# A planned decoder step: a margin before TensorE's side work, casts and copies fixed to ScalarE, more staging tiles, two stores on another queue

## The chip, the cores and the metric

The kernel runs on one core of a Trainium2 chip. A core has five engines, each with its own instruction queue, worked off in order: TensorE (PE, matrix multiplications into PSUM), VectorE (DVE), ScalarE (ACT), GpSimd (POOL) and SyncE (SP, which here only issues DMAs). The metric is the device time of one execution in microseconds (us). Before the change the median of three runs is 1080.3 us (1076.1 to 1082.3).

## The reference, cut to what matters

The reference computes one inference step of a two-layer recurrent decoder, in float32, for a prompt of 512 tokens and for 8 samples of one token each (520 columns in all), with a model width of 1024.

- Layer 0: RMSNorm, an input projection, and two branches. Branch A is a width-4 convolution, two block-diagonal gates and a linear recurrence (RG-LRU), times a SiLU gate. Branch B is a convolution with SiLU over x, B and C, a chunked state-space scan (SSD) with a step size dt per head, a SiLU gate z and a group norm. Both are concatenated and go through an output projection, then a residual add.
- Layer 1: RMSNorm, projections q, f, v and gate, a chunked linear-attention scan over 16 heads (HGRN2), a head norm, a SiLU gate, an output projection and a residual add.
- Each layer ends with a gated embedding:

```
def per_layer_embed(h, p, w_proj, w_gate):
    gate = jax.nn.sigmoid((h @ w_gate).astype(F32))
    return h + (gate * (p @ w_proj).astype(F32)).astype(h.dtype)
```

- A final RMSNorm gives y. Beside y the kernel returns the new recurrent and convolution states of prompt and samples.

## The kernel before, in words

**Layout.** Features lie on the 128 partitions and the 520 tokens (512 of the prompt, 8 samples) along the free dimension. A row of 128 features by 520 tokens is the unit of nearly all elementwise work.

**Multiplications.** Each float32 operand is split into two parts of a reduced type, a high one (cast) and a low one (the rest), and a product is three multiplications: high by high, high by low, low by high. A weight unit is 128 rows of contraction by 8, times 128 columns; `split_unit` makes its `whi` with a cast (by ScalarE or VectorE) and its `wlo` with a subtraction on VectorE. Both have two buffers. Weights come in by DMA two units at a time (`wraw`). `project` then runs one output row: for each of eight contraction steps a block of six multiplications, 48 in all, into a PSUM tile with two buffers, and then the row's evacuation.

**The planner.** The kernel's functions don't issue instructions; they record operations in a `Plan`. Main blocks (the projections) have a fixed order, and a position that grows by 0.668 us with each block. Everything else gets a due time: the position of its place in the code, shifted by a constant (`side(start, rate)`), and never later than what its main consumer needs. `Plan.order` then simulates all engines with a table of costs: an instruction becomes ready when its predecessors have ended (`release` adds `SYNC`, 0.12 us, between engines), and each engine takes the ready one that is due first. `copy` and `scaled` are recorded in two forms, one for ScalarE and one for VectorE, and the planner takes whichever engine comes free first. The result is a fixed order per engine. On the chip an engine that reaches an instruction whose operands are late stands still, and what is queued behind it waits too.

**TensorE's side work in layer 0.** Between the main blocks of the projections ax, xbc, z and ag stand:
- `gates(j)`: row j of xa, the convolution's result, is split into `xg`, and 12 multiplications with `gw` go into the PSUM tiles g;
- `ssd_start`: `dt_project` (multiplications, then transposes dtT), then on GpSimd a polynomial for the logarithm and the products dt and dA (tiles `htmp`, `dtt`), then the multiplications acs (cumulative sums) and the transposes acsT; `lru_out` transposes the last recurrence states (`ah`, from `ahs`);
- `ssd_chunk(g, c)`: for two groups and four chunks, transposes bt and xk, multiplications yd and yo, and the chunk's state st.

**Evacuation of ax and xbc.** `evac_raw` copies the PSUM row into a raw row (part of tile `bcs`), and the convolution then runs one ScalarE and three VectorE operations on it.

**The embeddings.** `embed(layer, ...)` multiplies p with `w_proj` into eight rows (pl), copies each into a staging tile and stores it to DRAM (`pl_d`) by SP; the rows are read back later. Four staging tiles take turns in both layers. Embedding 1 runs between the last projection of layer 0 (pg) and the first of layer 1 (f), beside the norm that makes layer 1's input (`xh`, `xl`). Its staging is the place `xa`, which holds 4160 columns of float32, and there are 8 x 520 such columns; later the same place takes the states of layer 1 (`l1c`).

**The end.** `layer1_end` runs the last projection in two halves of the tokens, then scales the transposed rows (`ytk`) by the final norm and stores y: four stores of 256 KB in the second half, and one for the samples, all issued by SP.

Of the kernel before, what the change touches and what calls it, by code (L numbers as in the profile page):

```python
# [25 lines left out]
N = T + NS  # L26
HN = N // 2
D = 1024
KT = D // 128
# [10 lines left out]
SYNC = 0.12  # L40
# [62 lines left out]
class Buf:  # L103


    def __init__(self, pool, shape, dt, tag, name, bufs, space, born):
        self.pool, self.shape, self.dt, self.tag, self.name, self.bufs, self.space = pool, shape, dt, tag, name, bufs, space
        self.born, self.acc, self.used, self.dead, self.real = born, [], [], None, None
        self.left, self.bank = 0, None
# [90 lines left out]
class Op:  # L200


    def __init__(self, plan, prio, i):
        self.plan, self.prio, self.i = plan, prio, i
        self.forms, self.preds, self.soft, self.succ, self.bufs = {}, {}, {}, [], {}
        self.size, self.cols, self.wait, self.ready, self.taken, self.main = 0, 0.0, 0, 0.0, None, False
        self.pinned = plan.pinned


class Plan:  # L210
# [3 lines left out]
    def __init__(self, engines, pools, banks):  # L214
        self.engines, self.pools, self.banks = engines, pools, banks
        self.ops, self.slots, self.pos, self.open, self.gate = [], defaultdict(list), 0.0, None, None
        self.shift, self.rate, self.pinned = 0.0, 0.0, False


    def tile(self, pool, shape, dt, tag, name, bufs=1, space=SBUF):  # L220
# [21 lines left out]
    @contextmanager  # L242
    def side(self, start=0.0, rate=0.0, pinned=False):

        keep = self.shift, self.rate, self.pinned
        self.shift, self.rate, self.pinned = start, rate, pinned
        yield
        self.shift, self.rate, self.pinned = keep

    @contextmanager  # L250
    def together(self, *views):
# [96 lines left out]
    def order(self):  # L348
# [17 lines left out]
        def release(op, t):  # L366
            todo = [(op, t)]
            while todo:
                p, t_ = todo.pop()
                for s, hard in p.succ:  # L370
                    if hard:
                        s.ready = max(s.ready, t_ + (SYNC if p.forms and not ("pe" in p.forms and "pe" in s.forms) else 0))
                    s.wait -= 1
                    if not s.wait:
                        offer(s, todo)

        def offer(s, todo):
            if not s.forms:
                todo.append((s, s.ready))
            for e in s.forms:  # L380
                heapq.heappush(pend[e], (s.ready, s.i, s))
# [63 lines left out]
        while left:  # L445
# [16 lines left out]
            calls, c, func = op.forms[e]  # L462
            for b in need(op):
                i = min(range(len(banks)), key=lambda i: banks[i])
# [8 lines left out]
            else:  # L473
                if e == "pe":

                    c = c + 0.003 * len(calls) if cols[int(t / 3.41333) - 1] >= 3060 else 2.0 * c
# [45 lines left out]
GATE_LATE, GATE_RATE, LRU_LATE, DT_LATE = -0.77, 1.03, 13.0, -5.19  # L522
SSD_LATE, SSD_C, SSD_G, SSD_RATE = -5.66, 3.04, 5.84, 0.14
# [7 lines left out]
def hybrid_decode_step_kernel(ctx: ExitStack, tc: tile.TileContext, I, O, mode="both"):  # L531
# [18 lines left out]
    plans = [Plan(engines, pools, [f"ax{i}" for i in range(4)])]  # L550
    act, dve, pool, pe, sp = (Engine(plans, k) for k in ("act", "dve", "pool", "pe", "sp"))
    side, block = (lambda *a, **k: plans[-1].side(*a, **k)), (lambda *a: plans[-1].block(*a))

    def new(pool_, shape, tag, name, bufs=1, dt=F32):
        return plans[-1].tile(pool_, shape, dt, tag, name, bufs, {"psm": PSUM, "psa": PSUM, "drp": DRAM}.get(pool_, SBUF))
# [7 lines left out]
    def grab(name):  # L563

        return new("psa", [128, 512], "ax", name)

    def halves(ap):
        return ap.rearrange("p (a b) -> p a b", a=2)

    def ps520(ps):  # L570
        return ps[:, :, :HN]
# [4 lines left out]
    def tt(out, a, b, op, eng=dve):  # L576
        eng.tensor_tensor(out=out, in0=a, in1=b, op=op)
# [13 lines left out]
    def copy(out, in_):  # L591

        plans[-1].record(("act", "copy", (out, in_), {}), ("dve", "tensor_copy", (out, in_), {}))
# [6 lines left out]
    def slot(tag, name, shape=None, dt=F32):  # L600
        return new("lay", shape or [128, KT, N], tag, name, dt=dt)
# [5 lines left out]
    groups, units, sec = [], [], {}  # L607
# [19 lines left out]
    def split_unit(u, hi=None, lo=None, eng=dve):  # L627
        g, s, uc, kk = units[u]
        if g not in raw_of:
            load_group(g)  # L630
        v = raw_of[g][:, :, s:s + uc]
        if hi is None:
            hi = new("wp", [128, 1024], "whi", f"whi{u}", 2, F32R)
            lo = new("wp", [128, 1024], "wlo", f"wlo{u}", 2, F32R)
        hv = hi[:, :kk * uc].rearrange("p (k c) -> p k c", k=kk)
        lv = lo[:, :kk * uc].rearrange("p (k c) -> p k c", k=kk)
        with side(*((plans[-1].shift, 0.0, True) if plans[-1].pinned else (-SPLIT_AHEAD,))):
            copy(hv, v)
            tt(lv, v, hv.bitcast(F32), SUB, eng)
        split_of[u] = (hv, lv)  # L640

# [61 lines left out]
    def project(u, m, pair, kmap, evac, name):  # L703
        project_both([(u, m, evac, name)], pair, kmap)
# [96 lines left out]
    def P1(r, n=1):  # L801
        return pt[:, 0, r:r + n]
# [62 lines left out]
    def embed(layer, PP, stg):  # L865
        def mk(j):
            def f(ps):
                s = stg[:, j % 4 * N:(j % 4 + 1) * N]
                copy(halves(s), ps520(ps))
                sp.dma_start(out=pl_d[layer][j], in_=s)  # L870
            return f

        for j in range(8):
            u, m = (sec["proj1"] + j // 4, j % 4) if layer else (sec["proj0"] + j // 2, j % 2) if j < 4 else (sec["proj0b"], j - 4)
            project(u, m, PP, [0, 1], mk(j), f"pl{layer}{j}")
# [164 lines left out]

    def evac_raw(ps, i, lc):
        raw = raws[i % 2]
        copy(halves(raw[:, 3:3 + N]), ps520(ps))
        pool.tensor_copy(lc, raw[:, T:T + 11])
        return raw

    xa, lt = slot("xa", "xa"), slot("z", "lt")
# [32 lines left out]
    def evac_ax(j):  # L1080
        def f(ps):
            raw = evac_raw(ps, j, LCa[:, :, j])
            conv(raw, xa[:, j, :T], P1(24 + j), P1(16 + j), P1(8 + j), P1(j), P1(32 + j))
            s = xa[:, j, T:]
            ts(s, LCa[:, 3:, j], P1(24 + j), MUL, P1(32 + j), ADD, pool)
            for k in (2, 1, 0):
                stt(s, SCa[:, :, k, j], P1(8 * k + j), s, MUL, ADD)
            for i in () if j == 0 else (0, 1) if j == 1 else (j,):
                with side(GATE_LATE, GATE_RATE):
                    gates(i)  # L1090
        return f

# [133 lines left out]
                lru(0)  # L1226
    with side(LRU_LATE):
        lru(4)
    with side(DT_LATE):
        ssd_start()  # L1230
        lru_out()

# [151 lines left out]

    for c in range(NCH):
        for g in range(2):
            with side(SSD_LATE + c * SSD_C + g * SSD_G, SSD_RATE):
                ssd_chunk(g, c)
    for g in range(2):
        with side(SSD_LATE + NCH * SSD_C):  # L1390
# [161 lines left out]
    with side(CONV_LATE):  # L1552
        conv_states()
    pp1 = slot("w", "pp1", [128, 4160], F32R)
    embed(1, split_p(pk1[:, :1024], pk1[:NS, 1024:1280], pp1[:, :4 * N].rearrange("p (k n) -> p k n", k=4), 1),
          slot("xa", "plt1", [128, 4 * N]))

    split_unit(sec["f0"], pp1[:, 2080:3104], pp1[:, 3104:4128])
    if mode == "both":
# [412 lines left out]
    def layer1_end(pl1, ytk, ytk4, keep, pre):  # L1972
# [7 lines left out]
        for j in range(2, 8):  # L1980
            t, o = keep[j // 2 - 1], j % 2 * 2048
# [40 lines left out]
        for half, (sl, blocks) in enumerate(HALVES):  # L2022
            psr = grab(f"ssf{half}")
            n, c0, nb = sl.stop - sl.start, blocks[0], len(blocks)
            for j in range(8):
                u = u0 + j
                hw, lw = split_of[u]
                ps = mmps(f"pg1{j}{half}")
                for k in range(8):
                    with block(True):  # L2030
                        for i, (w, x) in enumerate(((hw, xh), (hw, xl), (lw, xh))):
                            pe.matmul(ps[:, 0, :n], lhsT=w[:, k, :], rhs=x[:, k, sl],
                                      start=(k == 0 and i == 0), stop=(k == 7 and i == 2))
                    plans[-1].pos += 0.334
                evac(half, j, ps, psr)
            stt(ss[:, c0:c0 + nb], psr[:, 8 + c0:8 + c0 + nb], 1.0 / D, ss[:, c0:c0 + nb], MUL, ADD)
            for i in blocks:
                pool.tensor_tensor(out=ss[:, i:i + 1], in0=ss[:, i:i + 1], in1=nhalf[:, :1], op=ALU.pow)
            for i in blocks[:2]:
                for c in range(0, D, 512):  # L2040
                    y = ytk[:, i, c:c + 512]
                    scaled(y, y, ss[:, i:i + 1])
                    sp.dma_start(out=O["y_p"][0, i * 128:(i + 1) * 128, c:c + 512], in_=y)
        scaled(ytk4[96:], ytk4[96:], ss[96:, 4:5])
        sp.dma_start(out=O["y_s"].rearrange("b o d -> (b o) d"), in_=ytk4[120:])

    layer1_fast()
    layer1_end(slot("xa", "pl1"), slot("w", "ytk", [128, 4160])[:, :4 * D].rearrange("p (i d) -> p i d", i=4),
# [54 lines left out]
```

## Time and profile before

| | before |
|---|---|
| median of 3 runs | 1080.3 us (1076.1 to 1082.3) |
| profiled execution, its own time | 1080.04 us |
| its span, first to last instruction | 1078.3 us |
| mean granted TensorE clock | 0.989 |
| busy: TensorE / VectorE / ScalarE / GpSimd | 1046.1 / 778.2 / 507.6 / 140.2 us |
| moved by DMA | 138.43 MB, 128 GB/s |

How to read the profile: an engine's busy time doesn't say that it does useful work at full speed; beside it stands the clock that TensorE was granted (1.00 is full). Idle time is put down to what ended it ("releaser"), an engine and the tile that it wrote. Since the planner's loop issues everything, lines have one number (510) and tiles tell the work apart. A row of a window's view gives the window, its length, then busy time and count of TensorE, weight loads, VectorE, ScalarE and GpSimd, then the clock, the share of the DMA engines and GB/s. A queue with a small q (SPq, ACTq) is an engine's own DMA issues or sequencer.

### The profile page before, as it was taken

To read this page: it belongs to the slowest core of one execution; us is meant where nothing else is said; L and a number is where in the kernel's file an instruction comes from. 1 tells how busy PE (TensorE), PEld (TensorE's weight loads), DVE (VectorE), ACT (ScalarE), POOL (GpSimd) and SP (SyncE) were. 2 spreads that over 40 slices of the span, in tenths; PEclk is the share of its full clock that TensorE was granted. 3 is DMA by queue.
4 is the path that set the end of the run, shared out by engine and by line. 5 is a ranking of instruction groups with operands and counts; after the bars stand their busy time and mean duration, and the time that the engine had idled before them with its cause. 6 is when DMAs were issued, how large, how long until landed. Compare 5 with 4: busy or idle time off the path is not lost.

```text
span 1078.3 us, 21240 instructions
## 1 busy us (share of the span) xinstructions
PE 1046.1 (97%) x8595; PEld 1024.8 (95%) x8595; DVE 778.2 (72%) x1532; ACT 507.6 (47%) x1191; POOL 140.2 (13%) x241
## 2 busy tenths in 40 slices
PE   9999889999999999999999999999999999999995
PEld 8899889799999999999999999999999999999995
DVE  6899788999996656774858676575766757667853
ACT  6587464635474212352455445334463344642453
POOL 4636655110000000100000000000000000000000
PEclk9999899999999999999999999999999999999997
DMA  8712153344685234563433433342442433335311
GB/s 272 246 40 79 48 185 126 99 147 147 199 264 203 82 106 131 164 192 106 130 112 111 116 112 118 91 150 87 116 130 85 139 103 110 99 82 206 118 40 44
DMA packets 130466, 138.43 MB, mean 128 GB/s; under 512 B 13704, under 2 KB 111128, under 8 KB 130344
## 3 DMA queue, kind: packets, MB, share of 16 engines
q1 hardware_dynamic: 130136, 136.93, 41.1%
q8 instruction: 69, 1.13, 0.4%
q14 instruction: 37, 0.30, 0.1%
q0 software_dynamic: 224, 0.06, 0.0%
HBM read 111.71 MB, written 25.44 MB: 127 GB/s over the span
## 4 chain that ended last, share of the span: by engine, by line
PE 82%; DVE 6%; POOL 5%; DMA 3%; ACT 2%; issue 1%; POOLq 0%; DVEq 0%; ACTq 0%
PE o L510 11%; PE g L510 9%; PE f L510 9%; PE v L510 9%; PE q L510 9%; PE pg L510 7%; PE ag L510 4%; PE oa L510 4%; PE ob L510 4%; PE z L510 4%; PE xbc L510 2%; POOL htmp L510 2%; PE ax L510 1%; PE A L510 1%; PE kv L510 1%
## 5 line engine op out<-in xcount | busy, mean ns | idle before, releaser
L510 DVE TENSOR_TENSOR wlo<-wraw,whi 128x1024 fp32r<-128x1024 f32 (+1 forms) x143 | 173.5, 1213 | 4.2 <-ACT whi L510 2.4
L510 ACT CAST whi<-wraw 128x1024 fp32r<-128x1024 f32 (+1 forms) x67 | 69.5, 1037 | 126.8 <-PE q L510 41.2
L510 POOL TENSOR_TENSOR at__1569<-at__1569,nhalf 128x4 f32<-128x4 f32 (+1 forms) x24 | 20.7, 861 | 502.6 <-DVE at__1569 L510 502.6
L510 DVE CAST whi<-wraw 128x1024 fp32r<-128x1024 f32 x76 | 52.5, 691 | 38.5 <-PE f L510 13.2
L510 PE MATMUL g<-xh,whi 128*128 128x260 f32 x256 | 55.8, 299 | 0.0
L510 PE MATMUL q<-xh,whi 128*128 128x260 f32 x256 | 53.2, 289 | 0.0
L510 PE MATMUL o<-oh,whi 128*128 128x260 f32 x256 | 52.6, 286 | 0.0
L510 PE MATMUL v<-xh,whi 128*128 128x260 f32 x256 | 52.1, 285 | 0.0
L510 PE MATMUL v<-xh,wlo 128*128 128x260 f32 x256 | 51.6, 283 | 0.0
L510 PE MATMUL o<-oh,wlo 128*128 128x260 f32 x256 | 51.5, 283 | 0.0
L510 PE MATMUL g<-xh,wlo 128*128 128x260 f32 x256 | 51.5, 283 | 0.0
L510 PE MATMUL g<-xl,whi 128*128 128x260 f32 x256 | 51.5, 283 | 0.0
L510 PE MATMUL o<-ol,whi 128*128 128x260 f32 x256 | 51.5, 283 | 0.0
L510 PE MATMUL q<-xl,whi 128*128 128x260 f32 x256 | 51.5, 282 | 0.0
L510 PE MATMUL v<-xl,whi 128*128 128x260 f32 x256 | 51.4, 282 | 0.0
L510 PE MATMUL q<-xh,wlo 128*128 128x260 f32 x256 | 51.4, 282 | 0.0
L510 PE MATMUL f<-xh,whi 128*128 128x260 f32 x240 | 50.8, 293 | 0.0
L510 PE MATMUL f<-xl,whi 128*128 128x260 f32 x240 | 48.3, 283 | 0.0
L510 PE MATMUL f<-xh,wlo 128*128 128x260 f32 x240 | 48.2, 282 | 0.0
L510 DVE SCALAR_TENSOR_TENSOR l1a<-q,lbt,l1a 128x260 f32<-128x260 f32 (+1 forms) x32 | 14.0, 480 | 44.2 <-PE q L510 44.2
L510 DVE SCALAR_TENSOR_TENSOR l1c<-l1d,l1c 128x128 f32<-128x128 f32 x128 | 41.0, 347 | 0.6 <-ACT l1c L510 0.6
L510 PE MATMUL xbc<-xnh,whi 128*128 128x260 f32 x192 | 40.5, 294 | 0.0
(504 smaller groups left out, 3359.3 us busy)
## 6 DMA issues: line engine op xcount, KB each, us to landing
wraw<-in_c_w_in_dram SPq DMA_DIRECT2D x32, 1024.0 KB
wraw<-in_ab_w_in_dram SPq DMA_DIRECT2D x15, 1024.0 KB
wraw<-in_ab_w_out_dram SPq DMA_DIRECT2D x8, 1024.0 KB
wraw<-in_ple_gate_dram SPq DMA_DIRECT2D x8, 1024.0 KB
l1c<-in_state_c_dram SPq DMA_DIRECT2D x16, 512.0 KB
out_dram<-l1c SPq DMA_DIRECT2D x16, 512.0 KB
wraw<-in_c_w_out_dram SPq DMA_DIRECT2D x8, 1024.0 KB
pl<-pl_d SPq DMA_DIRECT2D x2, 2080.0 KB
```

Source lines behind the costliest of these rows:

```text
L510: getattr(f, name)(*a, **k)
```

## The change

Four things:

1. A new context, `later(spare)`. Operations recorded inside it carry `spare`, and when the planner works out when such an operation on TensorE is ready, it adds `spare` us for every predecessor that doesn't run on TensorE. The gates get 0.5, `ssd_start` and `lru_out` 4.0, and the SSD chunks 1.0.
2. In layer 0, from section ax2 up to (not including) pg0, the cast of each weight unit is recorded for ScalarE alone. That takes in ax2, proj0, proj0b, the xbc sections, z, ag, z1, out0a and out0b. The raw copy of `evac_raw` is for ScalarE alone, too.
3. `embed` takes turns over as many staging tiles as its place holds, and embedding 1 gets a place of eight; embedding 0 stays at four.
4. Of the last five stores of y, the second half of token block 3 and that of the samples are issued by ScalarE.

```diff
-        self.pinned = plan.pinned
+        self.pinned, self.spare = plan.pinned, plan.spare
...
+    @contextmanager
+    def later(self, spare):
+
+        keep, self.spare = self.spare, spare
+        yield
+        self.spare = keep
...
-                        s.ready = max(s.ready, t_ + (SYNC if p.forms and not ("pe" in p.forms and "pe" in s.forms) else 0))
+                        lag = SYNC if p.forms and not ("pe" in p.forms and "pe" in s.forms) else 0
+                        if "pe" in s.forms and p.taken != "pe":
+                            lag += s.spare
+                        s.ready = max(s.ready, t_ + lag)
...
-            copy(hv, v)
+            if sec["ax2"] <= u < sec["pg0"]:
+                act.copy(hv, v)
+            else:
+                copy(hv, v)
             tt(lv, v, hv.bitcast(F32), SUB, eng)
...
-                s = stg[:, j % 4 * N:(j % 4 + 1) * N]
+                i = j % (stg.shape[1] // N)
+                s = stg[:, i * N:(i + 1) * N]
...
-        copy(halves(raw[:, 3:3 + N]), ps520(ps))
+        act.copy(halves(raw[:, 3:3 + N]), ps520(ps))
...
-                with side(GATE_LATE, GATE_RATE):
+                with side(GATE_LATE, GATE_RATE), plans[-1].later(0.5):
                     gates(i)
...
-    with side(DT_LATE):
+    with side(DT_LATE), plans[-1].later(4.0):
         ssd_start()
         lru_out()
...
-            with side(SSD_LATE + c * SSD_C + g * SSD_G, SSD_RATE):
+            with side(SSD_LATE + c * SSD_C + g * SSD_G, SSD_RATE), plans[-1].later(1.0):
                 ssd_chunk(g, c)
...
-          slot("xa", "plt1", [128, 4 * N]))
+          slot("xa", "plt1", [128, KT * N]))
...
-                    sp.dma_start(out=O["y_p"][0, i * 128:(i + 1) * 128, c:c + 512], in_=y)
+                    (act if i == 3 and c else sp).dma_start(out=O["y_p"][0, i * 128:(i + 1) * 128, c:c + 512], in_=y)
...
-        sp.dma_start(out=O["y_s"].rearrange("b o d -> (b o) d"), in_=ytk4[120:])
+        act.dma_start(out=O["y_s"].rearrange("b o d -> (b o) d"), in_=ytk4[120:])
```

More of the change, by code (lines that the diff above doesn't have):

```diff
@@ L216, in __init__ @@
         self.ops, self.slots, self.pos, self.open, self.gate = [], defaultdict(list), 0.0, None, None
-        self.shift, self.rate, self.pinned = 0.0, 0.0, False
+        self.shift, self.rate, self.pinned, self.spare = 0.0, 0.0, False, 0.0
     def tile(self, pool, shape, dt, tag, name, bufs=1, space=SBUF):
```

## The prediction

> **What bounds the kernel now.** I read the page's engine shares first, then busy time by stage, then TensorE's waits, and last the stretches around each wait. All times are us, and nearly every instruction carries line 510, the one loop that issues the plan, so I go by tiles.
>
> ```profile
> PE 1046.1 (97%) x8595; PEld 1024.8 (95%) x8595; DVE 778.2 (72%) x1532; ACT 507.6 (47%) x1191; POOL 140.2 (13%) x241
> PE 82%; DVE 6%; POOL 5%; DMA 3%; ACT 2%; issue 1%; POOLq 0%; DVEq 0%; ACTq 0%
> ```
>
> TensorE is the bound: 97% busy, 82% of the chain that ended last. None of its multiplications goes away, so only three things can shorten the run: its waits, its slow-clock stretches, and the tail after its last instruction. TensorE's waits, longest first (what waited, for what; total, times, longest):
>
> ```profile
> PE acs L510 <- POOL dtt L510: 4.8, 1, 4.8
> PE ah L510 <- POOL ahs L510: 2.7, 1, 2.7
> PE pl L510 <- ACT plt L510: 2.1, 1, 2.1
> PE st L510 <- ACT bcs L510: 1.9, 1, 1.9
> ```
>
> The fifth group is the gate multiplications g, waiting in five places (the bracket is TensorE's idle time just before):
>
> ```profile
> 50.81 1.59 PE L510 MATMUL g<-xg,gw 128*128 128x260 f32 x11 [1.86 <-DVE xg L510]
> 55.62 1.58 PE L510 MATMUL g<-xg,gw 128*128 128x260 f32 x11 [0.21 <-DVE xg L510]
> 62.22 1.59 PE L510 MATMUL g<-xg,gw 128*128 128x260 f32 x11 [1.29 <-DVE xg L510]
> 95.52 0.39 PE L510 MATMUL g<-xg,gw 128*128 128x260 f32 x1 [0.79 <-ACT xg L510]
> 96.38 1.59 PE L510 MATMUL g<-xg,gw 128*128 128x260 f32 x11 [0.47 <-DVE xg L510]
> ```
>
> All but pl are side instructions of layer 0 that stand in TensorE's queue, in front of main blocks that could have run, before their operands are there. A wait also costs clock. Busy time by stretch (TensorE, weight loads, VectorE, ScalarE, GpSimd; then granted clock, DMA share, GB/s):
>
> ```profile
> 60.00:90.00 30.00, 28.71 (x237) 27.80 (x236) 29.43 (x59) 28.56 (x50) 10.99 (x16) 1.00 0.24 71
> 116.50:122.00 5.50, 5.50 (x25) 5.32 (x26) 3.09 (x7) 1.03 (x4) 4.45 (x16) 0.50 0.05 14
> 149.40:152.90 3.50, 3.50 (x18) 3.50 (x18) 1.83 (x7) 3.50 (x10) 1.49 (x3) 0.53 0.41 158
> 462.00:468.00 6.00, 6.00 (x38) 5.98 (x39) 5.39 (x9) 5.20 (x9) 0.00 (x0) 0.72 0.54 201
> 195.00:320.00 125.00, 124.39 (x1043) 118.90 (x1042) 118.95 (x234) 67.00 (x236) 7.43 (x6) 1.00 0.55 174
> ```
>
> The last row gives the full pace: 1043 in 125 is 8.34 per us, 0.12 each. Against it, 116.5 to 122 (behind the acs wait, clock 0.50) did 25 instead of 45.9, a loss of 20.9 x 0.12 = 2.5. Behind the ah wait: 18 instead of 29.2, a loss of 1.3. Behind the pl wait: 38 instead of 50, a loss of 1.4. The other waits are 1.9 and shorter and I charge them no clock.
>
> **The change, part by part.** I make the sum against the profiled execution: 1080.0, of which 1078.3 is the span and 1.7 lies around it. The median of the runs is 1080.3, so the two agree.
>
> *The margin of 4.0 for acs, acsT, dtT and ah.* The planner counts a TensorE instruction ready 4.0 later than its operands by its own clock, so it fills that time with main blocks. What is late is GpSimd's chain from dt to dA:
>
> ```profile
> 95.81 0.78 POOL L510 TENSOR_SCALAR dtt<-dtt 128x80 f32<-128x80 f32 x1 [0.18 <-DVE dtt L510]
> 116.07 0.35 POOL L510 TENSOR_TENSOR dtt<-dtt,hb 128x80 f32<-128x80 f32 x1
> ```
>
> From 95.81 to 116.42 it takes 20.6, and TensorE reached acs 4.8 too early. The margin on dtT delays chain and consumer alike; the one on acs takes 4.0 from the wait, leaving 0.8. So -4.0 (ends: 0 if GpSimd falls behind by as much again, -4.8 if it runs freer). A rest of 0.8 is below every wait behind which I counted slow matmuls, so the 2.5 goes too. The ah wait of 2.7 is inside the margin: -2.7 and -1.3 (ends: 0 and -4.0 together). What is queued behind acs and ah is main xbc work; what waits for their results is the SSD chunks, and these have time, as the next term shows.
>
> [...]
>
> *The margins of 0.5 (gates) and 1.0 (SSD chunks).* Each g wait shrinks by 0.5 at most: 1.86, 0.21, 1.29, 0.79, 0.47 (4.6) become 1.36, 0, 0.79, 0.29, 0 (2.4), so -2.2 (ends 0 and -4.6). The st wait of 1.9 becomes 0.9: -1.0 (ends 0 and -1.9). In exchange the side chains get longer. Serially that is at most 3 x 4.0 for ssd_start and, for each of four chunks, st and the next yo at 1.0 each: 8. Their consumers:
>
> ```profile
> L510 DVE SCALAR_TENSOR_TENSOR bx<-bx,dcol,yd x32: 333/342/346, 184.0 to 253.7; 128x128 f32<-128x128 f32 x32
> L510 DVE SCALAR_TENSOR_TENSOR bx<-bx,zs x8: 693/696/699, 278.6 to 332.7; 128x520 f32<-128x520 f32 x8
> ```
>
> The last chunk's output is written at 253.7 and first used at 278.6. These 25 hold both, 20, so I cost the longer chains at nothing; with that cover gone the price would be what exceeds 25.
>
> *Casts and raw copies fixed to ScalarE.* From 40 to 320 (busy us, mean ns):
>
> ```profile
> sum 280.00, PE 265.12 PEld 255.13 DVE 249.10 ACT 164.11 POOL 93.83; mean PE 37.87 PEld 36.45 DVE 35.59 ACT 23.44 POOL 13.40
> L510 DVE CAST whi<-wraw 128x1024 fp32r<-128x1024 f32 x20 | 13.8, 690 | 1.7 <-PE ag L510 0.8 <-PE z L510 0.5
> L510 ACT CAST whi<-wraw 128x1024 fp32r<-128x1024 f32 x16 | 16.7, 1043 | 0.6 <-PE oa L510 0.3 <-PE xbc L510 0.2
> L510 DVE TENSOR_TENSOR wlo<-wraw,whi 128x1024 fp32r<-128x1024 f32 x36 | 44.2, 1228 | 2.1 <-ACT whi L510 1.9
> L510 DVE CAST whi<-wraw x1: 689/689/689, 74.0 to 74.0; 128x1024 fp32r<-128x1024 f32 x1
> L510 DVE CAST whi<-wraw x2: 694/722/749, 81.5 to 102.9; 128x1024 fp32r<-128x1024 f32 x2
> L510 DVE COPY bcs<-ax x4: 687/690/692, 41.8 to 66.9; 128x520 f32<-128x520 f32 x4
> L510 DVE COPY bcs<-xbc x6: 692/699/701, 109.5 to 174.3; 128x520 f32<-128x520 f32 x6
> L510 ACT COPY bcs<-xbc x6: 570/594/596, 102.4 to 180.7; 128x520 f32<-128x520 f32 x6
> ```
>
> Twenty casts and ten copies move. VectorE loses 13.8 + 4 x 0.69 + 6 x 0.70 = 20.8 and falls from 249.1 to 228.3; ScalarE gains 20 x 1.04 + 10 x 0.59 = 26.8 and rises from 164.1 to 190.9 of 280. A faster TensorE needs VectorE to do the same work in less time, and the row from 195 to 320 has it at 118.95 of 125; the relief pays for that. A weight unit is 48 multiplications, 5.8; with two buffers a cast and its subtraction have that long, and need 1.04 + 1.23 = 2.3 instead of 0.69 + 1.23 = 1.9, so 3.5 of slack remain. Only from 60 to 90 does ScalarE lack room: 28.6 of 30, plus two casts (those at 74.0 and 81.5) and the later two of the four ax copies, 3.3, gives 31.9. I charge the 1.9 that is too much as +2 (ends 0, if the planner moves other copies to VectorE, and +3.3).
>
> *Eight staging tiles for embedding 1.* With four, the fifth copy waits until the first store has landed:
>
> ```profile
> 447.89 2.88 PE pl L510 x24
> 451.72 9.40 DMA pl_d<-plt
> 461.22 0.59 ACT L510 COPY plt<-pl 128x520 f32<-128x520 f32 x1 [3.30 <-DMA pl_d<-plt]
> 461.87 1.83 PE pl L510 x12
> 463.69 12.92 PE f L510 x96
> 458.02 0.76 DVE L510 SCALAR_TENSOR_TENSOR n<-h,pt,acc 128x520 f32<-128x520 f32 x1
> 462.99 0.69 DVE L510 TENSOR_TENSOR xl<-sqt,xh 128x520 fp32r<-128x520 f32 x1
> ```
>
> The wait (2.1) and its slow clock (1.4) go: -3.5. Next late is the norm that feeds f: the ScalarE casts of xh, now queued behind the blocked plt copy, come free with it; VectorE then needs 0.76 + 0.69 = 1.45 for each of eight steps where f needs 12 x 0.12 = 1.44. They run level, so I give back 0.5: -3.0 (ends -2.1 and -3.5). The eight stores stay on SP in the same order and no longer wait for a tile; the state loads that reuse their place (l1c) wait for the last of them in both kernels.
>
> *Two y stores from ScalarE.*
>
> ```profile
> 1069.24 1.67 DVE L510 TENSOR_SCALAR ytk<-ytk,ss 128x512 f32<-128x512 f32 x3 [0.32 <-POOL ss L510]
> 1069.75 2.94 SPq L510 DMA_DIRECT2D out_dram<-ytk  x5
> 1071.00:1072.00 1.00, 0.00 (x0) 0.00 (x0) 0.00 (x0) 0.00 (x0) 0.00 (x0) 0.50 0.94 359
> ```
>
> SP issues five stores in 2.94, 0.59 each, until 1072.7. With three on SP, and ScalarE's last one after VectorE's end at 1070.9, both end at 1071.5: 1.2 at most. But the transfers already fill the DMA engines from 1071 on (0.94 busy), so I take -0.3 (ends 0 and -1.2). A second issuing queue appears in no row; nothing is queued behind ScalarE's two issues, so I bound its own cost by 0 and their 1.2, and take 0.
>
> [...]
>
> *New places, new waits.* The order of every engine is drawn up afresh, and side work may meet late operands elsewhere. From below: 0.6 idle in 125, the row from 195 to 320, which is also full of side work. From above: the 14.0 of acs, ah, st and g coming back. The margins speak for the lower end; I take +3.
>
> The sum: -4.0 - 2.5 - 2.7 - 1.3 - 2.2 - 1.0 - 3.0 - 0.3 = -17.0, then +2 and +3: -12.0. That gives 1068.0.
>
> **The rivals.** *All of it comes through* (0.17). Every wait goes and nothing new appears: 4.8 + 2.5 + 4.0 + 4.6 + 1.9 + 3.5 + 1.2 = 22.5 off: 1057.5. For it: VectorE's relief also brings xg and GpSimd's inputs earlier. Against: 0.5 doesn't cover g waits of 1.86 and 1.29.
>
> *The margins don't do what they say* (0.15). They are measured on the planner's clock, and the chip's lag comes from queues that the new order changes too; the layer-0 waits come back in other places in full. Then only embedding 1 and the tail remain: 1080.0 - 3.3 = 1076.7. For it: GpSimd's 20.6 for a chain of small operations shows how far lags can grow.
>
> *ScalarE becomes what TensorE waits for* (0.11), the rival on the other side. The casts now stand in a strictly ordered queue behind instructions that wait:
>
> ```profile
> ACT smp L510 <- DMA smp<-in_state_b_ssm_dram: 13.5, 5, 4.7
> ```
>
> A wait of 4.7 exceeds the slack of 3.5 by 1.2. If all twenty moved casts met such a one, TensorE would lose 24: 1080.0 - 17.0 + 24 = 1087. It decides, as slower, once the twenty together lose over 22, that is 1.1 each. Against it: sixteen casts run there on ScalarE today and TensorE's list of waits has none for whi.
>
> **How the numbers follow.** My forecast has 0.57, with a range of its own from 1062 to 1074; the rivals have 0.17, 0.15 and 0.11. Within 0.5% (5.4) is about what a measurement of this kernel can't tell from no change. The forecast and the first rival are faster by more: 0.74. The second is within: 0.15. The third is slower: 0.11. The range from 1058 to 1080 takes in the second rival and most of the first, and leaves out the slower one and a little below.
>
> **What would show it.** Right: the acs wait at about 0.8 with a clock of 1.00 after it; no ah and no pl wait; the g waits near 2.4 in sum; f taking about 11.6 instead of 12.9; VectorE near 228 in layer 0's stretch, ScalarE near 191; TensorE idle for some 12 less. Wrong: a TensorE wait for whi or for a raw copy on ScalarE of more than 2 in sum between 60 and 320; a new wait over 2 anywhere with a clock near 0.5 behind it; or a gap before b_norm's first use of bx, the longer SSD chains showing.

## The result, and the profile after

The changed kernel takes 1069.1 us (median of 6 runs, 1066.0 to 1071.2) against 1080.8 (6 runs, 1076.1 to 1082.3). The ratio is 0.9904, 95% interval 0.988 to 0.9927, so 7.9 to 13.0 us were won. The profiled execution took 1067.7, its span is 1066.0 and its mean granted clock 0.995 (before 1080.0, 1078.3, 0.989). The forecast was 1068.0.

The page's engine shares and the shares of the chain of waits, after:

```profile
PE 1040.6 (98%) x8595; PEld 1019.7 (96%) x8595; DVE 766.0 (72%) x1520; ACT 528.3 (50%) x1205; POOL 138.4 (13%) x241
PE 80%; DVE 6%; DMA 4%; POOL 4%; ACT 4%; issue 1%; SPq 0%; POOLq 0%; ACTq 0%; DVEq 0%
```

TensorE is still the bound. Its waits after (what waited, for what; total, times, longest):

```profile
PE acs L520 <- POOL dtt L520: 3.7, 1, 3.7
PE g L520 <- DVE xg L520: 3.0, 4, 1.7
...
PE sbt L520 <- DVE acy L520: 1.6, 1, 1.6
...
PE ax L520 <- DVE htmp L520: 0.9, 1, 0.9
PE st L520 <- ACT bcs L520: 0.8, 1, 0.8
...
PE st L520 <- DVE acy L520: 0.3, 1, 0.3
```

The waits at ah and pl are gone. The one at acs went from 4.8 to 3.7 only. sbt, the transpose at the start of the samples, has grown from 0.2; it got no margin.

Busy time by stretch, after (TensorE, weight loads, VectorE, ScalarE, GpSimd; clock, DMA share, GB/s):

```profile
128.40:134.40 6.00, 5.91 (x37) 5.91 (x38) 5.21 (x10) 2.54 (x7) 3.20 (x5) 0.72 0.01 3
60.00:90.00 30.00, 29.71 (x244) 29.20 (x245) 28.97 (x62) 28.93 (x47) 10.92 (x18) 1.00 0.24 71
40.00:320.00 280.00, 269.55 (x2219) 259.32 (x2219) 243.50 (x462) 188.74 (x458) 91.46 (x164) 0.99 0.47 151
453.00:462.00 9.00, 9.00 (x77) 9.00 (x77) 8.98 (x15) 5.94 (x10) 0.00 (x0) 1.00 0.66 221
```

Behind acs the clock still falls: 37 multiplications in 6.0 us where 50 fit, 1.6 lost (before 2.5). From 60 to 90 TensorE is busier than before (29.71 against 28.71), and in embedding 1 the clock is now 1.00.

Where the time went, by the start of each stage's last or first multiplication:

| mark (us from the span's start) | before | after | difference |
|---|---|---|---|
| last of ax | 93.0 | 88.4 | -4.6 |
| last of xbc | 180.4 | 171.9 | -8.5 |
| first of oa (end of z, ag, z1) | 304.7 | 297.9 | -6.8 |
| last of layer 0's pg | 447.6 | 440.8 | -6.8 |
| first of f | 463.5 | 454.3 | -9.2 |
| last of the first row of f | 475.6 | 464.9 | -10.7 |
| last ssf (final norm) | 1067.5 | 1056.0 | -11.5 |
| span | 1078.3 | 1066.0 | -12.3 |

So layer 0 gained 8.5 up to the end of xbc and 6.8 up to oa, embedding 1 gained 3.9, the rest 1.6. Each column is one execution; the 1.7 between xbc and oa is less than two executions of one kernel order differ by (see e3 and e4 below).

### The profile page after: what moved, and what is told of

Read it like the earlier page. It is cut to its first block, busy times and chain, and to the rows that moved or that the text cites. A ratio compares the mean times of both kernels' runs of the same rounds, so it can differ in the third digit from the quotient of the medians.

```text
span 1066.0 us, 21247 instructions
## 1 busy us (share of the span) xinstructions
PE 1040.6 (98%) x8595; PEld 1019.7 (96%) x8595; DVE 766.0 (72%) x1520; ACT 528.3 (50%) x1205; POOL 138.4 (13%) x241
## 4 chain that ended last, share of the span: by engine, by line
PE 80%; DVE 6%; DMA 4%; POOL 4%; ACT 4%; issue 1%; SPq 0%; POOLq 0%; ACTq 0%; DVEq 0%
PE o L520 11%; PE g L520 9%; PE f L520 9%; PE pg L520 9%; PE v L520 9%; PE q L520 9%; PE oa L520 4%; PE ob L520 4%; PE ax L520 2%; PE pl L520 2%; PE xbc L520 2%; PE z L520 1%; POOL htmp L520 1%; PE kv L520 1%; PE A L520 1%; DVE wlo L520 1%
## 5 line engine op out<-in xcount | busy, mean ns | idle before, releaser
L520 ACT CAST whi<-wraw 128x1024 fp32r<-128x1024 f32 (+1 forms) x87 | 90.4, 1039 | 126.4 <-PE q L520 41.3
L520 DVE CAST whi<-wraw 128x1024 fp32r<-128x1024 f32 x56 | 38.7, 691 | 35.6 <-PE f L520 11.9
```

Source lines behind the costliest of these rows:

```text
L520: getattr(f, name)(*a, **k)
```

## The experiments

All ratios are to the kernel before, run beside it on the same chip. There it took 1080.0 (e1 to e4), 1078.9 (e5 to e8) and 1079.1 (e9 to e12). A list of waits and a row of a stretch come from one execution, which can lie off the median: that of e7 took 1085.7 and that of e1 1075.2, each the slowest of its runs, and that of e5 1068.8.

| run | what it has | median | ratio, 95% interval |
|---|---|---|---|
| e1 | part 1 (margins) | 1072.6 | 0.9923 [0.9898, 0.9948] |
| e2 | part 2 (casts, copies) | 1071.7 | 0.9930 [0.9907, 0.9953] |
| e3 | part 3 (eight tiles) | 1077.3 | 0.9972 [0.9955, 0.9988] |
| e4 | part 4 (stores) | 1078.7 | 0.9982 [0.9968, 0.9997] |
| e5 | parts 2, 3, 4 | 1071.6 | 0.9935 [0.9910, 0.9959] |
| e6 | part 2, casts alone | 1077.6 | 0.9988 [0.9971, 1.0005] |
| e7 | part 2, copies alone | 1079.6 | 1.0011 [0.9992, 1.0030] |
| e8 | all, 9.0 on acs | 1068.3 | 0.9903 [0.9880, 0.9925] |
| e9 | none, order drawn afresh | 1087.8 | 1.0080 [1.0048, 1.0111] |
| e10 | part 2, order drawn afresh | 1074.9 | 0.9969 [0.9947, 0.9990] |
| e11 | all, order drawn afresh | 1069.2 | 0.9904 [0.9882, 0.9925] |
| e12 | all, three margins wider | 1068.4 | 0.9904 [0.9879, 0.9929] |

**The parts one by one.** Four runs each have one part of the diff and nothing else.

e1 (margins):

```diff
-            with side(SSD_LATE + c * SSD_C + g * SSD_G, SSD_RATE):
+            with side(SSD_LATE + c * SSD_C + g * SSD_G, SSD_RATE), plans[-1].later(1.0):
...
```

> Only the margins (0.5, 4.0, 1.0); casts, copies, staging and stores as before. Theory (the margins bring layer 0's gain): the acs, ah, st and g waits shrink as in the changed kernel, layer 0 ends some 5 to 8 us earlier, the pl wait of 2.1 us stays, 1072 to 1075 us in the profiled execution. Rival (the relief of VectorE brings it): the waits come back elsewhere, within 2 us of before.

e2 (casts and copies):

```diff
-            copy(hv, v)
+            if sec["ax2"] <= u < sec["pg0"]:
+                act.copy(hv, v)
+            else:
+                copy(hv, v)
...
-        copy(halves(raw[:, 3:3 + N]), ps520(ps))
+        act.copy(halves(raw[:, 3:3 + N]), ps520(ps))
```

> Only the casts and raw copies fixed to ScalarE. Theory: VectorE loses about 20 us of busy time before 320 us and ScalarE gains about 25, but TensorE's waits for acs, ah, g and st, which come from GpSimd's chain and from side work queued too early, stay at 10 us or more in sum: within 3 us of before. Rival (the relief brings layer 0's gain): 5 to 8 us faster. Second rival (ScalarE is short of room from 60 to 90 us): a wait for whi or bcs appears, slower by 2 us or more.

e3 (staging tiles):

```diff
-                s = stg[:, j % 4 * N:(j % 4 + 1) * N]
+                i = j % (stg.shape[1] // N)
+                s = stg[:, i * N:(i + 1) * N]
...
-          slot("xa", "plt1", [128, 4 * N]))
+          slot("xa", "plt1", [128, KT * N]))
```

> Only the eight staging tiles of embedding 1. Theory: the wait of 2.1 us for plt and the slow clock behind it go, the f stage starts 2.1 to 2.4 us earlier and ends 3.5 to 4 us earlier, everything before 440 us is as before: 3.5 to 4 us off the span. Rival (the norm takes the wait's place): TensorE waits for xh or xl instead, and less than 2 us are gained.

e4 (stores):

```diff
-                    sp.dma_start(out=O["y_p"][0, i * 128:(i + 1) * 128, c:c + 512], in_=y)
+                    (act if i == 3 and c else sp).dma_start(out=O["y_p"][0, i * 128:(i + 1) * 128, c:c + 512], in_=y)
...
-        sp.dma_start(out=O["y_s"].rearrange("b o d -> (b o) d"), in_=ytk4[120:])
+        act.dma_start(out=O["y_s"].rearrange("b o d -> (b o) d"), in_=ytk4[120:])
```

> Only the two y stores issued by ScalarE. Theory: the time from TensorE's last instruction to the end of the span falls from about 10 us by 0.3 to 0.8 us, nothing else changes. Rival (transfers set the end, or the second queue costs something): 0, or longer.

By the medians they bring 7.4, 8.3, 2.7 and 1.3, together 19.7 where the whole brings 11.7. So the parts overlap, and part 2, which I had costed at a loss of 2, brings about as much alone as the margins do (their intervals overlap). The 2.7 of part 3 is less than the 3.5 to 4 expected, which its interval (1.3 to 4.9) still takes in. With the margins alone the ah wait is gone and sbt waits 1.6 already, but acs still waits 4.6 and pl 1.8; the first of oa came 3.4 earlier (301.3), not 5 to 8.

e3 and e4 have the order of the kernel before, instruction for instruction, on TensorE, VectorE, ScalarE and GpSimd. So they measure parts 3 and 4 in one order, and show what an order fixes: the waits at acs (4.8), ah (2.7) and st (1.9) are the same in all three executions. What an order leaves open differs: g waits 4.6, 4.6 and 3.3 in sum (before, e3, e4), the start of ax 0.3, 0.3 and 1.9, and the first of oa stands at 304.7, 304.8 and 307.8.

TensorE's longest waits in the run with part 2 alone:

```profile
PE acs L510 <- POOL dtt L510: 7.0, 1, 7.0
PE g L510 <- DVE xg L510: 3.2, 3, 2.4
```

The next three, ssf 1.9, warm 1.1 and pT 1.1, stand outside layer 0's side work and hardly change from kernel to kernel. The waits at ah, st and pl are gone without any margin and without more tiles, while acs has grown to 7.0. The pl wait went because a store landed sooner; ScalarE's timeline in the same run:

```profile
453.98 0.60 ACT L510 COPY plt<-pl 128x520 f32<-128x520 f32 x1 [0.59 <-DMA pl_d<-plt]
```

It is the sixth copy of plt, as the one with 3.30 in the kernel before. So from the end of the second copy (446.9) to the landing of its store it took 7.1, where it had taken 9.8 before (451.39 to 461.22). With the eight tiles alone the gain is embedding 1's, and f runs at the full pace of 0.12 for each multiplication (chain of waits, start and length):

```profile
461.33 10.78 PE f L510 x90
```

The stores' part is barely measured (interval 0.3 to 3.5). The time from ssf to the end of the span is 10.5 there, 10.0 in the changed kernel and 10.8 before; but part 2 alone, with the stores as before, has 10.1. Over all profiles it lies between 10.0 and 11.2 with the part and between 10.1 and 10.8 without.

**What part 2 does, and what the margins add beside it.** e5 is the changed kernel without `later`. e6 has only the casts of e2's diff, e7 only its copies.

```diff
-                with side(GATE_LATE, GATE_RATE), plans[-1].later(0.5):
+                with side(GATE_LATE, GATE_RATE):
...
-    with side(DT_LATE), plans[-1].later(4.0):
+    with side(DT_LATE):
...
```

> The changed kernel without its margins: parts 2, 3 and 4 only. Theory: the margins and the relief of VectorE remove the same waits of layer 0, so that beside part 2 the margins are worth 1 to 3 us (g waits 3.0 with them and 3.2 without, acs 3.7 against 7.0): 1070 to 1072, and the acs wait at about 7 with a slow clock behind it. Rival: the margins add nothing at all beside part 2 (what they take from acs they give back at sbt, 1.6, and by a later start of GpSimd's chain): 1069, level with the changed kernel, or faster.

> Only the casts of layer 0's weight units are fixed to ScalarE; raw copies, margins, staging and stores as before. Theory one, VectorE's freed time counts: the casts free 13.8 to 14 of it and the copies 7, so this alone brings two thirds of the 8.3 of both, 5 to 6: 1074 to 1075, and the ah and st waits shrink. Theory two, the raw copy is the first link of the chain that ends in the gates' operands and in GpSimd's inputs, and the casts have slack: this alone brings 2 at most, 1078 to 1080.

> Only the raw copies of ax and xbc are fixed to ScalarE; casts, margins, staging and stores as before. Theory one, VectorE's freed time counts: about 7 of VectorE's time, a third of what both free, so 2 to 3 of the 8.3: 1077 to 1078. Theory two, the chain from the raw copy counts: 6 or more, 1072 to 1074. If neither this run nor the casts alone brings much, the two need each other.

Without margins the kernel takes 1071.6, as the theory had it, with 7.1 at acs. Margins are worth some 3 beside the other parts (0.9935 against 0.9904) and 7.4 alone. The intervals of the two ratios overlap, but e8, which has the margins (9.0 on acs) and ran beside e5, took 1065.6 to 1068.8 in six runs against 1068.7 to 1073.0. e5 has the order of e2, instruction for instruction, so parts 3 and 4 bring nothing that can be told beside part 2 (0.9935 against 0.9930).

Casts alone and copies alone bring nothing that can be told from zero, while both together bring 8. Layer 0's stretch in the runs with casts alone, copies alone and both:

```profile
40.00:320.00 280.00, 266.64 (x2168) 256.99 (x2167) 240.66 (x456) 182.42 (x434) 97.46 (x168) 0.98 0.45 144
```

```profile
40.00:320.00 280.00, 262.90 (x2107) 252.30 (x2106) 242.11 (x441) 158.80 (x405) 91.92 (x167) 0.96 0.44 138
```

```profile
40.00:320.00 280.00, 269.24 (x2211) 260.20 (x2210) 240.86 (x456) 189.82 (x462) 79.62 (x166) 0.98 0.47 148
```

VectorE is busy for 240.7, 242.1 and 240.9 in the stretch, but the stretch holds different amounts of work: 2168, 2107 and 2211 multiplications. Over the whole program, in the same order of runs (778.2 in the kernel before):

```profile
PE 1046.1 (97%) x8595; PEld 1024.9 (95%) x8595; DVE 767.9 (71%) x1521; ACT 526.8 (49%) x1204; POOL 141.9 (13%) x241
PE 1049.2 (97%) x8595; PEld 1027.4 (95%) x8595; DVE 778.6 (72%) x1530; ACT 507.3 (47%) x1195; POOL 138.8 (13%) x241
PE 1043.1 (98%) x8595; PEld 1023.3 (96%) x8595; DVE 763.4 (71%) x1515; ACT 529.6 (50%) x1210; POOL 125.3 (12%) x241
```

So copies alone don't relieve VectorE at all: of the 37 casts of weight units up to oa the planner gave it 27 there, after 20 before. e7 is therefore no test of theory one; it speaks against theory two, in the one order that it has. e6 speaks against theory one as it was sized, since 10.3 of the 14.8 freed by both brought 1.2 and not 5 to 6. That VectorE's load has a share in it stays open: among the orders without margins, the less VectorE is busy, the shorter the time (e2 763.4, e10 766.6, e6 767.9, before 778.2, e7 778.6, e9 783.0), though not in proportion.

What also differs is where TensorE meets late operands: casts alone wait 5.9 at g, 3.8 at acs and 2.5 at ah; copies alone 5.4 at acs, 4.3 at g, 2.6 at oa and 2.4 at yd. Two explanations were left: the case that the expectation names last, that the two need each other, and a third theory: an edit that changes the planner's choices in layer 0 makes it draw up all engines' orders afresh, and each order has its own waits.

**The order drawn afresh.** Three kernels, before, part 2 alone and all parts, differ from themselves only here:

```diff
-SYNC = 0.12
+SYNC = 0.13
```

> The kernel before with one number of the planner's clock changed from 0.12 to 0.13 (what it adds between engines), which draws up the order of all engines afresh and is no improvement of anything. Theory: an order drawn up afresh moves the layer 0 waits by several us by itself, to either side, and much of what the parts bring one by one is that; then this kernel is off by 3 to 8 from the kernel before, with other waits. Rival: the gains of the parts are their own, and this kernel stays within 2 of the kernel before, with the waits at acs, ah, st and g.

> Part 2 alone (casts and copies on ScalarE), with the planner's clock at 0.13 instead of 0.12. Theory, an order drawn afresh counts: it stands apart from part 2 alone (1071.7) by 3 or more, and most likely slower, at 1074 to 1080, as casts alone and copies alone did. Rival, casts and copies together remove the waits by what they do: 1070 to 1073 again, with no ah and no st wait.

> The changed kernel with the planner's clock at 0.13 instead of 0.12. Theory, the margins are what makes the result hold when the order is drawn afresh: within 2 of the changed kernel, 1067 to 1071. Rival, its order is as much a draw as the others: off by 3 to 8, 1072 to 1077.

The kernel before loses 8.7 (1087.8 against 1079.1), a little more than the theory's bound of 8. The redrawn order also gives VectorE more to do (28 of the 37 casts, 783.0 in all), so it isn't neutral in that. Its waits then:

```profile
PE acs L510 <- POOL dtt L510: 9.1, 1, 9.1
PE ax L510 <- ACT htmp L510: 4.6, 1, 4.6
PE g L510 <- DVE xg L510: 3.0, 2, 2.1
PE ah L510 <- POOL ahs L510: 3.0, 1, 3.0
PE st L510 <- ACT bcs L510: 1.9, 1, 1.9
```

Part 2 alone loses 3 to 4 (1074.9 against 1071.7; 0.9969 against 0.9930, whose intervals just overlap), and ah is back:

```profile
PE acs L510 <- POOL dtt L510: 3.8, 1, 3.8
PE g L510 <- DVE xg L510: 3.8, 3, 3.2
PE ah L510 <- POOL ahs L510: 2.7, 1, 2.7
```

The changed kernel doesn't move (0.9904 both times), and its list keeps its shape:

```profile
PE acs L520 <- POOL dtt L520: 4.5, 1, 4.5
PE g L520 <- DVE xg L520: 3.0, 3, 2.4
...
PE ax L520 <- DVE htmp L520: 1.2, 1, 1.2
...
PE sbt L520 <- DVE acy L520: 1.0, 1, 1.0
```

So an edit of no substance can move a kernel without margins by as much as part 2 is worth, and the one with margins held. e8 and e12 below, with other margins beside the same parts, have two more orders and the same ratio, 0.9903 and 0.9904. These are few draws: they show that the spread exists, not how wide it is. It fits them that the margins narrow it, but that isn't shown. How much of part 2's 8.3 is its own stays open, with e10's 4.2 and e2's 8.3 as two draws of it.

**The wait at acs.** e8 gives acs and acsT 9.0 instead of 4.0:

```diff
         ps = grab("acs")
-        with block():
+        with plans[-1].later(9.0), block():
...
         ps = grab("acsT")
-        with block():
+        with plans[-1].later(9.0), block():
```

> The changed kernel with a margin of 9.0 instead of 4.0 on acs and acsT alone. Theory: TensorE's wait at acs (3.7 there) comes from the planner's clock running ahead of GpSimd's chain by a roughly fixed amount, so 5.0 more margin takes the wait and the slow matmuls behind it (37 in 6.0 instead of 50, 1.6): 1064, acs wait 0. Rival: the chain slips along with the new order, or the chunks behind acsT become what TensorE waits for (st, yd, sbt): 1068 to 1070, and the wait is found again there.

The time is that of the changed kernel (1068.3), as the rival said. TensorE's waits there:

```profile
PE g L520 <- DVE xg L520: 2.9, 4, 1.7
PE yd L520 <- DVE wsl L520: 2.1, 1, 2.1
...
PE acs L520 <- POOL dtt L520: 1.8, 1, 1.8
```

With 5.0 more margin TensorE reached acs 5.7 later (130.46 against 124.75, each the start less the wait), but GpSimd's chain ended 3.8 later (132.2 against 128.4). The chain slips along. Why is seen in the kernel before. GpSimd's timeline there, and then VectorE's (start, duration):

```profile
111.16 1.35 POOL L510 TENSOR_SCALAR htmp<-htmp 128x80 f32<-128x80 f32 x1
112.60 0.52 POOL L510 TENSOR_TENSOR htmp<-htmp 128x80 f32<-128x80 f32 x1
113.21 0.41 POOL L510 TENSOR_SCALAR htmp<-htmp 128x80 f32<-128x80 f32 x1
113.70 0.35 POOL L510 TENSOR_TENSOR htmp<-htmp 128x80 f32<-128x80 f32 x1
114.14 0.41 POOL L510 TENSOR_SCALAR htmp<-htmp 128x80 f32<-128x80 f32 x1
```

```profile
111.02 1.23 DVE L510 TENSOR_TENSOR wlo<-wraw,whi 128x1024 fp32r<-128x1024 f32 x1 [0.17 <-ACT whi L510]
112.16 0.75 DVE L510 SCALAR_TENSOR_TENSOR bcs<-bcs,pt 128x512 f32<-128x512 f32 x1
117.63 0.29 DVE L510 COPY at__1569<-acs 128x128 f32<-128x128 f32 x1 [4.72 <-PE acs L510]
```

A step that took 1.35 beside VectorE's work takes 0.41 once VectorE, too, stands before acs. Over eight profiles (before, after, e1, e2, e8, e9, e11, e12) I took the 23 steps on 128x80 of each chain and, from VectorE's rows, what share of the step VectorE was busy:

| VectorE busy during the step | TENSOR_SCALAR: count, mean | TENSOR_TENSOR: count, mean |
|---|---|---|
| under 30% | 29, 0.40 us | 34, 0.35 us |
| 30 to 80% | 9, 0.71 | 15, 0.65 |
| over 80% | 50, 0.93 | 47, 0.75 |

So TensorE's stop speeds up what it waits for: the main work stops, VectorE runs dry, and the chain runs at twice the pace (0.40 and 0.35 a step instead of 0.93 and 0.75). It is VectorE that counts, not main work at large: with VectorE busy for under 30% of a step, the steps of before and after average 0.34 to 0.42 whether TensorE is busy meanwhile (over 80%, 6 steps) or idle (under 30%, 13), and 0.35 to 0.43 with ScalarE busy (11) or idle (6). A margin fills the same time with main work, VectorE stays busy, and the chain takes longer. In e8 it starts 0.7 later than in the changed kernel and, with the same 44 operations, takes 3.1 longer: 1.9 more for the 23 steps (16.3 against 14.4) and 1.2 for the other 21.

From the kernel before to the changed one it is something else that grows. The 23 steps take 14.4 in both. But between them GpSimd does 21 other operations that take 9.3, most of them the samples' (csm) and row copies (LCb), where it had 7 that took 2.1; its idle time within the chain falls by 3.6 in exchange. Two of them in the changed kernel, one beside VectorE's work and one with VectorE idle:

```profile
123.43 0.65 POOL L520 TENSOR_TENSOR csm<-htmp,pt 128x8 f32<-128x8 f32 x1
...
127.92 0.20 POOL L520 TENSOR_TENSOR csm<-csm 128x8 f32<-128x8 f32 x1
```

**All remaining waits.** e12 has the 9.0 of e8 and two wider margins:

```diff
-                with side(GATE_LATE, GATE_RATE), plans[-1].later(0.5):
+                with side(GATE_LATE, GATE_RATE), plans[-1].later(2.0):
...
-        with side(SMP_LATE + g * 4 * SMP_J):
+        with side(SMP_LATE + g * 4 * SMP_J), plans[-1].later(2.5):
```

> The changed kernel with wider margins: 9.0 on acs and acsT, 2.0 instead of 0.5 on the gates, 2.5 on the start of the samples (sbt). Theory: the waits left in layer 0 of the changed kernel are g 3.0, sbt 1.6 and acs 3.7 with 1.6 of slow clock; the gates and sbt go, acs falls to 1.8 as in the run with 9.0 on acs alone: 1069.1 less 3 to 6, 1063 to 1066. Rival: the chains that get longer come out late elsewhere (the gates' results are what the recurrence, GpSimd and the transposes ah wait for), 1067 to 1071.

```profile
PE ax L520 <- DVE htmp L520: 2.6, 1, 2.6
PE g L520 <- DVE xg L520: 2.5, 1, 2.5
...
PE ah L520 <- POOL ahs L520: 1.8, 1, 1.8
PE xbc L520 <- DVE wlo L520: 1.6, 3, 0.7
```

acs and sbt no longer wait, and the stretch from 40 to 320 holds 2255 multiplications (after 2219; 36 more, some 4 us of work). Yet the time is 1068.4, not to be told from the changed kernel. Those 36 are net of the new waits at ah (1.8, the rival's) and for the weights' low parts (1.6), and before the stretch this execution lost 2.6 at 29 us, ahead of anything that the margins touch. By the profiles oa starts 2.9 earlier (295.0 against 297.9), the last ssf 1.8 earlier, and the span is 0.7 shorter, for the tail took 11.2 instead of 10.0; these are single executions. Neither this nor e8 nor e11 can be told from the changed kernel.

## Why the prediction was right, and where it was not

The median is 1.1 from the forecast, but that is in part luck, since errors cancel in it: too much was expected at acs, and charges for ScalarE and for new waits were too high. By the profiles, in us:

| term | predicted | measured |
|---|---|---|
| acs wait | -4.0 | -1.1 |
| clock behind acs | -2.5 | -0.9 |
| ah wait and clock | -4.0 | -4.0 |
| g waits | -2.2 | -1.6 (4.6 to 3.0) |
| st wait | -1.0 | -0.8 (1.9 to 1.1) |
| ScalarE too full, 60 to 90 | +2 | 0 |
| new waits | +3 | +2.0 (sbt 0.2 to 1.6, ax 0.3 to 0.9) |
| layer 0 in sum | -8.7 | -6.4 by these, -6.8 by the marks |
| embedding 1 | -3.0 | -3.9 |
| layer 1 | 0 | -0.8 |
| tail | -0.3 | -0.8 (not resolved) |
| sum | -12.0 | -12.3 |

Waits at g and ax differ by more than 1 between executions of one order (e3, e4 and before), so the rows for g, new waits, layer 1 and the tail are no finer than that.

**The step on acs failed.** It said that the margin "takes 4.0 from the wait, leaving 0.8" and that the slow clock behind it goes. The timelines after show the chain's ends and the wait, GpSimd first, then TensorE:

```profile
104.22 2.00 POOL L520 TENSOR_SCALAR dtt<-dtt 128x80 f32<-128x80 f32 x1 [5.09 <-DVE dtt L520]
...
128.08 0.35 POOL L520 TENSOR_TENSOR dtt<-dtt,hb 128x80 f32<-128x80 f32 x1
```

```profile
128.49 0.43 PE L520 MATMUL acs<-dtt,triu 128*128 128x64 f32 x2 [3.74 <-POOL dtt L520]
```

TensorE reached acs 13.1 later than before (124.75 against 111.66), and the chain ended 12.0 later: it began 8.4 later and took 24.2 instead of 20.6. So against the chain's start TensorE came 4.7 later, about the margin, and the longer chain took 3.6 of that back. I had kept this as the end of the term ("0 if GpSimd falls behind by as much again") and not taken it, since I held the chain's 20.6 for a property of the chain. It isn't: here GpSimd did 7.2 more of other work between the steps, and e8 shows that the pace of the steps, too, hangs on what the other engines do meanwhile (16.3 for the 23 with VectorE busy for 75% of their time, 14.4 here with 62%).

**The valuation of part 2 failed.** I costed it as load on ScalarE, +2, and its relief as only paying for a faster TensorE. No crowding shows, and alone the part brings 8.3 in one order and 4.2 in another. Nor did the relief come in the size given: VectorE fell to 243.5, not 228.3. The stretch holds more work (2219 multiplications after 2166), and the planner moved other operations to VectorE, above all scalings of the samples (smp, 28 after 17, 4.8 us); up to the first of oa VectorE is relieved of 10.1 and not 20.8. ScalarE rose to 188.7, near the 190.9 computed. What I left out is that any change of the planner's choices draws up the whole order again. I had this in the "+3", as a cost of the margins' sort; e9 shows that a redrawing alone can cost almost three times that.

**The margins do what they say** in the weaker sense: g, st and ah fell by about what was stated. That isn't theirs alone: with the margins alone g still waits 3.6 and st 1.4, and part 2 without margins has g at 3.2 and no wait at st or ah. What I didn't foresee is that with them the time held in the four orders tried (the changed kernel, e8, e11, e12). The room of 25 for the longer chunk chains held: the last yd product is now added by 241.7 and the first use of bx with zs is at 268.6, 27 apart.

**The embedding term was too small**, by 0.9, and 3.9 lies outside its ends (2.1 to 3.5). Of the 0.9, 0.5 is what I gave back for the norm; the other 0.4 isn't accounted for; with part 3 alone (e3) the gain from oa to the first row of f is the same 3.9. The chain of waits after has f at full pace:

```profile
454.44 10.79 PE f L520 x90
```

I also misread the row: five copies ran before the blocked one, so it was the sixth copy that waited, for the second store. And e2 shows that the wait hangs on the landing of that store as much as on the number of tiles: with four tiles the sixth copy waits 0.59 for it there, after 3.30 before, and TensorE has no wait at pl.

**The stores** issue from two queues, in 2.31 on SP and 1.08 on ScalarE. SP's three took more than the 1.8 that 0.59 each would give:

```profile
1057.60 2.31 SPq L520 DMA_DIRECT2D out_dram<-ytk  x3
1058.44 1.08 ACTq L520 DMA_DIRECT2D out_dram<-ytk  x2
```

SP's issue is shorter by 0.63 than the 2.94 before. Whether the end moved by that can't be told from the scatter of the tails.

**The rivals.** ScalarE as the bound is out: the only wait of TensorE for whi that is listed in a kernel with the casts moved is 0.2, in e12. VectorE does wait longer for whi before its subtractions (7.7 in all, 2.4 before), but of that TensorE sees little: at most the 1.6 for wlo in e12. That the margins shift waits to other places is half true: it holds for acs and sbt.

## What to carry to other kernels

Where a planner fixes the order, judge an edit against redrawn orders too, not against one order alone: change a number that means nothing, and see how far the time moves. First see whether the edit changes the order at all; where it doesn't (e3, e4), it can be compared directly. A margin ahead of a consumer is worth its own length only if the producer's pace doesn't hang on the consumer's standing still (here 5.0 more at acs took 1.9 from the wait, 3.7 to 1.8); look at how fast the producer's steps run during the wait, and at what else it does between them. Compare an engine's load over the same work, not over the same stretch of time. And gains of parts measured one by one needn't add up: here both large parts removed some of the same waits (19.7 alone, 11.7 together).

## What the runs showed of the hardware

**GpSimd beside VectorE.** The same step on 128x80 takes 0.35 to 0.40 on average with VectorE busy for under 30% of it and 0.75 to 0.93 with VectorE busy for over 80% (table above; spans on GpSimd are rough). By what means VectorE's work slows it isn't shown by these runs. Most of VectorE's work beside these steps has two inputs (TENSOR_TENSOR and SCALAR_TENSOR_TENSOR, 78.3 of 91.0 us in the eight profiles); the two steps that ran wholly beside a copy (bcs<-xbc, one input) took 0.41 (before) and 0.35 (e1), as with VectorE idle, too few to separate the cases.

**The clock falls after short waits, but not after each.** I charged no clock to waits of 1.9 or less. In e8, behind the acs wait of 1.81 and behind the yd wait of 2.06 (windows as above):

```profile
134.30:136.30 2.00, 2.00 (x11) 2.00 (x10) 1.70 (x5) 1.97 (x6) 0.82 (x2) 0.50 0.00 0
177.70:179.70 2.00, 2.00 (x16) 1.76 (x15) 2.00 (x7) 0.64 (x2) 2.00 (x6) 1.00 0.20 26
```

Behind the shorter wait the clock is halved (0.50), behind the longer one it is full (1.00). The length of one wait alone doesn't decide it; what does isn't settled by these runs.
